# The first two vectors of the adaptive norm: the weights as stationary operand of TensorE, the two conditioning vectors moving, and sixteen places for weight tiles

## Chip, core and metric

The program runs on one core of one Trainium2 chip. The metric is the device time of one execution in microseconds (us). Each engine of the core (TensorE, called PE; its weight loads, PEld; VectorE, DVE; ScalarE, ACT; GpSimd, POOL) takes its instructions in a fixed order, and the SyncE queue (SP) issues the DMAs in a fixed order too: a DMA that has to wait holds up all DMAs behind it.

## What is computed

The reference is a two-layer backbone over 1024 latent tokens and 256 context tokens with 1024 channels. Every sub-layer starts with an RMS norm whose shift and scale come from a conditioning vector. Cut to the part that matters here:

```python
silu_c = jax.nn.silu(c)                # latent tokens, 1024 values
silu_cc = jax.nn.silu(c_ctx)           # context tokens, 1024 values
mod   = silu_c  @ ada_w[i] + ada_b[i]  # ada_w[i]: 1024 x 6144
mod_c = silu_cc @ ada_w[i] + ada_b[i]
sh_m, sc_m, g_m, sh_f, sc_f, g_f = jnp.split(mod, 6, axis=-1)
h = modulate(rmsnorm(x, norm_mix_w[i]), sh_m, sc_m)   # h * (1 + scale) + shift
...
y, y_c = ab_mixer(h, hc, ...)
```

Nothing of layer 0 behind its first norm can start before its scale (vector 1 of the six) and shift (vector 0) are there. Each of these two vectors is a product of two rows of 1024 values with a 1024 x 1024 piece of `ada_w[0]`, 4 MB in float32.

## The kernel before

Activations lie with channels on the 128 partitions and tokens along the free axis, in eight tiles `xT[0..7]`. The large products run in three passes of a split (`whi`, `wlo` times `hh`, `hl`).

The start of the program is what the change touches. `body` calls `setup`, then makes a generator `ada(s, a, 0, [1, 0], "pe")` for vectors 1 and 0, and loads ten row tiles of `x` and `ctx` (`load_x`, 128 tokens x 1024 channels, 512 KB each), taking one step of the generator after each. After row tiles 3, 7 and 9 a block of tokens is turned: `turn_x` transposes, for each of the eight channel groups, the block's row tiles on PE into PSUM (`xt`), and ACT (even groups) and DVE (odd groups) copy the result to `xT`. Then `rstd` squares the eight groups on ACT, adds them on DVE, and sums over partitions with float32 matmuls against one column of ones (`ss`, 128x1). Blocks 0, 1 and 2 hold 512, 512 and 256 tokens.

A step of the generator loads one tile of weights (`adaw`, 128 input channels x 1024 output channels, 512 KB) and multiplies it with the two vectors `cs`. Eight steps (`k` = 0..7) make one vector, so there are sixteen tiles. Before the change, the four columns `cs[:, k, 2 - 2v : 6 - 2v]` (two of them zero) are the stationary operand and half a weight tile moves, 512 columns: the result `adaps` is four rows of 512. It is copied to SBUF (`adarow`), turned by four small transposes (`adat`), sorted (`adasum`), and added to the bias, which gives `mod`.

The weight tiles and the row tiles of x lie in the sixteen places of `hslot` (tags `h0k`, `h1k`; one buffer each), which later hold the normalised activations `hh`, `hl`. Row tile `i` takes place `h(i%2)(i//2)`, so that the row tiles fill places `h00` to `h14`; the weight tiles before take the six places with numbers 5, 6 and 7. A tile framework orders the instructions of each engine by its own simulation and adds the waits.

Behind this stage stands `norm` of block 0 (`spread`: the matmul `rbc`; then per channel group `nt` on DVE, `hh` on ACT with the shift as bias, `hl` on DVE), and behind it the first products `qk`.

Of the kernel before, what the change touches and what calls it, by code (L numbers as in the profile page):

```python
# [11 lines left out]
F32 = mybir.dt.float32  # L12
# [8 lines left out]
P = 128  # L21
D = 1024
KT = D // P
# [46 lines left out]
def psum(s, tag, name=None):  # L70

    if tag == "s" and s.single:
        return s.pp.tile([P, 512], F32, name=name or tag, tag="q", bufs=4)
    if tag != "s":
        return s.ps.tile([P, 512], F32, name=name or tag, tag=tag, bufs=2 if tag == "t" else 1)
    if s.half is None:
        pair = psum2(s, name)
        s.half = pair[:, 512:]
        return pair[:, :512]
    half, s.half = s.half, None  # L80
    return half


def psum2(s, name=None):

    s.half = None
    return s.pp.tile([P, 1024], F32, name=name or "pair", tag="s", bufs=2)
# [25 lines left out]
def setup(s, a):  # L113
    nc, cp = s.nc, s.cp
    cp.tile([P, 24], F32, name="pad")
    s.ident = cp.tile([P, P], F32, name="ident")
    make_identity(nc, s.ident)
    s.ones = cp.tile([P, P], F32, name="ones")
    nc.gpsimd.memset(s.ones, 1.0)
    s.half_neg = cp.tile([P, 16], F32, name="half_neg")  # L120
    nc.gpsimd.memset(s.half_neg, -0.5)


    flat = lambda ap, n: bass.AP(tensor=ap.tensor, offset=ap.offset, ap=[[P, n], [1, P]])
    r0 = s.xp.tile([16, P], F32, name="r0")
    nc.sync.dma_start(r0[0:8, :], flat(a["c"], 8))
    nc.sync.dma_start(r0[8:16, :], flat(a["c_ctx"], 8))
    s.cs = s.hc.tile([P, KT, 6], F32, name="cs")
    nc.gpsimd.memset(s.cs, 0.0)
    pt = psum(s, "t", "setup")  # L130
    nc.tensor.transpose(pt[:, :16], r0, s.ident[:16, :16])
    nc.scalar.activation(s.cs[:, :, 2:4], pt[:, :16].rearrange("p (s k) -> p k s", s=2), AF.Silu)

    r1 = s.xp.tile([P, P], F32, name="r1")
    nc.gpsimd.memset(r1, 0.0)
    rows = [("nmw", a["norm_mix_w"], 16), ("nfw", a["norm_ffn_w"], 16), ("dbf", a["cd_decay_b_fwd"], 2),
            ("dbb", a["cd_decay_b_bwd"], 2), ("hnw", a["cd_head_norm_w"], 1), ("sgb", a["ab_sgu_b"], 4)]
    at = 0
    for name, ap, n in rows:
        nc.sync.dma_start(r1[at:at + n, :], flat(ap, n))  # L140
        at += n
    r2 = s.xp.tile([96, P], F32, name="r2")
    nc.sync.dma_start(r2, flat(a["ada_b"], 96))
    pt = psum(s, "t", "setup")
    nc.tensor.transpose(pt[:, :P], r1, s.ident)
    nc.tensor.transpose(pt[:, P:P + 96], r2, s.ident[:96, :96])
    s.cols = cp.tile([P, 41], F32, name="cols")
    nc.vector.tensor_copy(s.cols, pt[:, :41])
    s.adab = cp.tile([P, 96], F32, name="adab")
    nc.vector.tensor_copy(s.adab, pt[:, P:P + 96])  # L150
    at = 0
    s.col = {}
    for name, ap, n in rows:
        s.col[name] = s.cols[:, at:at + n]
        at += n
    s.mod = [cp.tile([P, 48, 2], F32, name=f"mod{l}") for l in range(2)]
    s.acol = [[cp.tile([P, KT, 2], F32, name=f"acol{l}{j}") for j in range(2)] for l in range(2)]


def ada(s, a, l, vecs, eng):  # L160

    nc = s.nc
    for i, m in enumerate(vecs):
        if eng == "pe":
            acc = psum(s, "o", "adaps")
        else:
            acc = s.adap.tile([P, 2, D], F32, name="adaacc", tag="adaacc", bufs=1)
        for k in range(KT):  # L170
            if eng == "pe":
                w = hslot(s, (8 * i + k) % 2, 5 + (8 * i + k) // 2 % 3, dt=F32, name="adaw")
            else:
                w = s.adap.tile([P, D], F32, name="adaw", tag="adaw", bufs=s.nada)
            nc.sync.dma_start(w, a["ada_w"][l, k * P:(k + 1) * P, D * m:D * (m + 1)])
            for v in range(2):
                c = s.cs[:, k, v + 2:v + 3]
                if eng == "pe":

                    nc.tensor.matmul(acc[:4, :], s.cs[:, k, 2 - 2 * v:6 - 2 * v], w[:, 512 * v:512 * (v + 1)],  # L180
                                     start=k == v == 0, stop=k == KT - 1 and v == 1)
                elif k == 0:
                    nc.scalar.mul(acc[:, v], w, c)
                elif eng == "dve":
                    nc.vector.scalar_tensor_tensor(acc[:, v], w, c, acc[:, v], ALU.mult, ALU.add)
                else:
                    prod = s.adap.tile([P, D], F32, name="adaprod", tag="adaprod", bufs=2)
                    nc.scalar.mul(prod, w, c)
                    nc.gpsimd.tensor_tensor(acc[:, v], acc[:, v], prod, ALU.add)
            if k < KT - 1:  # L190
                yield 1
        sums = s.adap.tile([P, 2, 8], F32, name="adasum", tag="adasum", bufs=1)
        if eng == "pe":
            row = s.adap.tile([4, 512], F32, name="adarow", tag="adarow", bufs=1)
            nc.vector.tensor_copy(row, acc[:4, :])
            pt = psum(s, "m", "adat")
            for q in range(4):
                nc.tensor.transpose(pt[:, 4 * q:4 * q + 4], row[:, P * q:P * (q + 1)], s.ident[:4, :4])
            nc.vector.tensor_copy(sums.rearrange("p v (h q) -> p q h v", h=2), pt[:, :16].rearrange("p (q h v) -> p q h v", q=4, h=2))
        else:  # L200
            for v in range(2):
                for q in range(2):
                    pt = psum(s, "mo"[q], "adat")
                    for j in range(4):
                        c = 4 * q + j
                        nc.tensor.transpose(pt[:, j * P:(j + 1) * P], acc[:, v, c * P:(c + 1) * P], s.ident)
                    nc.vector.tensor_reduce(sums[:, v, 4 * q:4 * q + 4], pt.rearrange("p (j q) -> p j q", j=4),
                                            AX.X, ALU.add)
        nc.vector.tensor_tensor(s.mod[l][:, 8 * m:8 * (m + 1), :], sums.rearrange("p v c -> p c v"),
                                s.adab[:, 48 * l + 8 * m:48 * l + 8 * (m + 1)].rearrange("p (c o) -> p c o", o=1)  # L210
                                .to_broadcast([P, 8, 2]), ALU.add)
        yield 1
# [1533 lines left out]
def hslot(s, x, k, shape=(P, T), dt=F32R, name="hslot"):  # L1746

    return s.hm.tile(list(shape), dt, name=name, tag=f"h{x}{k}", bufs=1)
# [73 lines left out]
def body(ctx, tc, a, out, dbg=None):  # L1822
# [26 lines left out]
    with P_("hc", side="left") as s.hc:  # L1849
# [6 lines left out]
        with ExitStack() as es:  # L1856
# [4 lines left out]
            with R("ld") as ld, R("np0") as s.np_:  # L1861
                s.xp = s.adap = ld
                setup(s, a)
                jobs = [q(0), k(0)]
                s.bg = ada(s, a, 0, [1, 0], "pe")
                xin, r = [], {}
                for i in range(TA // P):
                    xin.append(load_x(s, a, i))
                    tick(s)
                    if i == 7:  # L1870
                        acol(s, 0, 0)
                    if i in (3, 7, 9):
                        blk = BLK[(i - 2) // 3]
                        turn_x(s, xin, xT, blk)
                        r[blk] = rstd(s, xT, blk)
                tick(s, 3)
                ws = proj_w(s, a, jobs)
                drain(s)
                hT = alloc_hc(s)
                s.hc.tile([P, 16], F32, name="pad")  # L1880
                proj_t(s, a, hT, jobs, pre=lambda blk: norm(s, xT, hT, 0, 0, blk, r[blk]), ws=ws)
                spill(s, xT, xd[0])
            with R("ad") as s.adap:
                s.nada = 2
                rbd = s.dp.tile([120, 64, P], F32, name="rbd")

                def prepare():
                    rows = bias_rows(s, a, s.adap, rbd)
                    for i, _ in enumerate(ada(s, a, 0, [2, 3, 4], "dve")):
                        if i % 3 == 2:  # L1890
                            next(rows, 0)
                        yield 1

                s.bg = prepare()
                gmlp(s, a, hT, mixd, q(1), values_b(s, a, hT, vb, 0))
                drain(s)
                acol(s, 0, 1)
# [258 lines left out]
```

## Time and profile before

| what | value |
|---|---|
| time, median of 3 runs | 2769.5 us (2765.0 to 2773.36) |
| the profiled execution, its own time | 2768.02 us |
| its span, first to last instruction | 2766.2 us |
| mean granted TensorE clock | 0.985 |
| DMA, mean over the span | 131 GB/s |
| first `hh` of block 0 (ACT) starts | 59.08 us into the span |

The span is the program's own; the 1.8 us beside it lie around it. A line of the timeline gives start, duration (of the first start to the last end, where several are merged), engine, line, operation, written tile, read tiles, shapes, and how many. A float32 matmul appears as two records, since PE makes two passes; a transpose as one. The 40 slices of the page are too coarse for a stage of 60 us, so the prediction reads windows of a few us.

### The profile page before, as it was taken

The page shows a single profiled execution, that of the slowest core. Times are in us where ns is not written, and L with a number is a line of the kernel's source. Part 1 is how long each engine was busy: PE and PEld are TensorE (multiplying, and loading weights), DVE is VectorE, ACT ScalarE, POOL GpSimd, SP SyncE. Part 2 cuts the span into 40 slices and gives each one's busy share as a digit, 9 for nine tenths or more (in the row PEclk, how much of TensorE's full clock was granted, in tenths as well). Part 3 has the DMA queues.
Part 4 walks back from the last instruction along what each step waited for, and adds up shares of the span by engine and source line. Part 5 has one row for each costly group of instructions (what it writes and reads, how often), then busy time and mean ns, then how long its engine had stood idle before and what let it go on. Part 6 is the DMA issues. An engine that isn't in the chain of part 4 may idle for free.

```text
span 2766.2 us, 39949 instructions
## 1 busy us (share of the span) xinstructions
PE 2654.0 (96%) x14447; PEld 2255.3 (82%) x14447; DVE 1944.8 (70%) x3508; ACT 1022.7 (37%) x2244; POOL 426.4 (15%) x389
## 2 busy tenths in 40 slices
PE   8999899999999999999999988999999999999998
PEld 3889798778888888888888877788877888888887
DVE  4655677776867778778878774756677666677666
ACT  3442466554533333333111145565244222222222
POOL 0000122221212122211000020312002112121111
PEclk9999999999999999999999989999999999999999
DMA  8545665766234434346644242542641111211112
GB/s 312 149 151 140 184 174 138 237 191 195 107 119 137 133 130 139 128 130 227 240 160 149 65 146 86 150 138 71 193 140 46 61 46 46 61 47 61 55 52 84
DMA packets 281590, 361.02 MB, mean 131 GB/s; under 512 B 38008, under 2 KB 198961, under 8 KB 281393
## 3 DMA queue, kind: packets, MB, share of 16 engines
q1 hardware_dynamic: 281393, 358.46, 41.3%
q8 instruction: 115, 1.88, 0.3%
q14 instruction: 82, 0.67, 0.1%
HBM read 259.03 MB, written 95.94 MB: 128 GB/s over the span
## 4 chain that ended last, share of the span: by engine, by line
PE 68%; DVE 14%; DMA 6%; ACT 5%; issue 4%; POOL 2%; SPq 1%; DVEq 0%; POOLq 0%; ACTq 0%
PE dn L49 6%; PE dn L50 6%; PE dn L51 6%; PE qp L49 6%; PE qp L50 6%; PE qp L51 6%; DVE adaacc L231 2%; DMA adaw<-in_ada_w_dram 2%; DVE wlo L57 2%; PE o L1159 2%; PE pt L1129 1%; ACT whi L56 1%; PE ho L49 1%; PE qk L49 1%; PE sp L1070 1%
## 5 line engine op out<-in xcount | busy, mean ns | idle before, releaser
L56 ACT CAST whi<-wraw 128x512 fp32r<-128x512 f32 (+1 forms) x451 | 292.1, 661 | 888.5 <-PE dn L50 375.0
L57 DVE TENSOR_TENSOR wlo<-wraw,whi 128x512 fp32r<-128x512 f32 (+1 forms) x451 | 355.9, 796 | 192.2 <-ACT whi L56 186.7
L351 DVE SCALAR_TENSOR_TENSOR xT<-dn,mod,xT 128x512 f32<-128x512 f32 (+1 forms) x448 | 303.7, 686 | 132.0 <-PE dn L51 130.3
L558 POOL TENSOR_TENSOR wraw<-wraw 128x512 f32<-128x512 f32 x160 | 230.1, 1438 | 897.1 <-DVE wlo L57 710.2
L231 DVE SCALAR_TENSOR_TENSOR adaacc<-adaw,cs,adaacc 128x512 f32<-128x512 f32 x196 | 165.7, 865 | 19.6 <-DMA adaw<-in_ada_w_dram 19.0
L49 PE MATMUL dn<-hhi,whi 128*128 128x512 f32 (+1 forms) x416 | 157.2, 378 | 0.0
L51 PE MATMUL dn<-hhi,wlo 128*128 128x512 f32 (+1 forms) x416 | 156.8, 377 | 0.0
L50 PE MATMUL dn<-hlo,whi 128*128 128x512 f32 (+1 forms) x416 | 156.7, 377 | 0.0
L49 PE MATMUL qp<-hh,whi 128*128 128x512 f32 x320 | 125.3, 391 | 6.8 <-DVE hu L626 6.8
L51 PE MATMUL qp<-sums,wlo 128*128 128x512 f32 x320 | 125.3, 391 | 1.9 <-DVE wlo L57 1.9
L49 PE MATMUL qp<-sums,whi 128*128 128x512 f32 x320 | 124.8, 390 | 0.1
L51 PE MATMUL qp<-hh,wlo 128*128 128x512 f32 x320 | 124.6, 389 | 0.0
L50 PE MATMUL qp<-sums,whi 128*128 128x512 f32 x320 | 124.5, 389 | 0.0
L50 PE MATMUL qp<-hl,whi 128*128 128x512 f32 x320 | 124.5, 389 | 0.0
L626 DVE TENSOR_TENSOR hu<-qp,hu 128x512 f32<-128x512 f32 x120 | 82.5, 687 | 54.2 <-PE qp L51 53.0
L49 PE MATMUL dn<-hslot,whi 128*128 128x512 f32 x288 | 112.3, 390 | 1.1 <-DVE xT L351 1.1
L51 PE MATMUL dn<-hslot,wlo 128*128 128x512 f32 x288 | 112.2, 390 | 0.0
L50 PE MATMUL dn<-hslot,whi 128*128 128x512 f32 x288 | 112.2, 390 | 0.0
L1086 POOL TENSOR_SCALAR y<-y,sst 128x768 f32<-128x768 f32 (+2 forms) x80 | 71.9, 900 | 259.2 <-DVE sst L1085 123.8
L49 PEld LDWEIGHTS dn<-hhi,whi 128*128 128x128 f32 x416 | 78.2, 188 | 14.8 <-ACT hhi L56 0.3
L50 PEld LDWEIGHTS dn<-hlo,whi 128*128 128x128 f32 x416 | 78.2, 188 | 14.4
L49 PE MATMUL cp<-hc,whi 128*128 128x256 f32 x320 | 89.9, 281 | 0.0
(677 smaller groups left out, 7682.2 us busy)
## 6 DMA issues: line engine op xcount, KB each, us to landing
adaw<-in_ada_w_dram SPq DMA_DIRECT2D x112, 256.0 KB, 2.8
wraw<-in_ffn_w_gate_dram SPq DMA_DIRECT2D x44, 512.0 KB, 3.8
wraw<-in_ffn_w_up_dram SPq DMA_DIRECT2D x44, 512.0 KB, 3.8
wraw<-in_ffn_w_down_dram SPq DMA_DIRECT2D x42, 512.0 KB, 3.4
adaw<-in_ada_w_dram SPq DMA_DIRECT2D x40, 512.0 KB, 5.7
xd<-xT SPq DMA_DIRECT2D x24, 640.0 KB, 3.9
xT<-xd SPq DMA_DIRECT2D x48, 256.0 KB, 4.2
wraw<-in_ab_w_in_dram SPq DMA_DIRECT2D x20, 512.0 KB, 5.7
```

The source lines that it names most:

```text
L49: nc.tensor.matmul(out, wh, xh, start=start, stop=False)
L50: nc.tensor.matmul(out, wh, xl, start=False, stop=False)
L51: nc.tensor.matmul(out, wl, xh, start=False, stop=stop)
L56: s.nc.scalar.copy(hi, src)
L57: (s.nc.gpsimd if eng == "pool" else s.nc.vector).tensor_tensor(lo, src, f32(hi), ALU.subtract)
L231: nc.vector.scalar_tensor_tensor(acc[:, v], w, c, acc[:, v], ALU.mult, ALU.add)
L351: s.nc.vector.scalar_tensor_tensor(xT[k][:, o:o + n], ps, s.mod[l][:, 8 * vec + k, sel:sel + 1], xT[k][:, o:o + n], ALU.mult, ALU.add)
L558: sub = lambda out, x, y: feed.s.nc.gpsimd.tensor_tensor(out, x, y, ALU.subtract)
L626: add = lambda out, x, y: nc.vector.tensor_tensor(out, x, y, ALU.add)
L1070: nc.tensor.matmul(sp[:, o:o + n], qq[:, x, :], kk[:, t0:t0 + n], start=x == 0, stop=x == 1)
L1086: nc.gpsimd.tensor_scalar(y[:, :256 + xn], y[:, :256 + xn], st[:, 5:6], 1.0, ALU.mult, ALU.mult)
L1159: nc.tensor.matmul(o_ps[:, ba * P:bz * P], vv[:n, kt, :], at(x, sl)[:n, 0, ba:bz, :].rearrange("p b q -> p (b q)"), start=q == 0 and x == ...
```

## The change

In `ada` with `eng == "pe"`, each 128x128 piece of the weight tile becomes the stationary operand and the two columns of `cs` move. The result has output channels on the partitions and the two vectors beside each other, as `mod` wants it, so that the copy, the four transposes and the sorting go. Vector 1 accumulates in PSUM bank "m", vector 0 in "o". The weight tiles take all sixteen places, in order; the first ten of them are the places of the ten row tiles of x. The clearing of `cs` goes.

```diff
-    nc.gpsimd.memset(s.cs, 0.0)
...
         if eng == "pe":
-            acc = psum(s, "o", "adaps")
+            acc = psum(s, "mo"[i % 2], "adaps")[:, :16].rearrange("p (c v) -> p c v", c=8)
...
             if eng == "pe":
-                w = hslot(s, (8 * i + k) % 2, 5 + (8 * i + k) // 2 % 3, dt=F32, name="adaw")
+                w = hslot(s, k % 2, (8 * i + k) // 2 % 8, dt=F32, name="adaw")
...
-            for v in range(2):
+            for c in range(8 if eng == "pe" else 0):
+                nc.tensor.matmul(acc[:, c, :], w[:, P * c:P * (c + 1)], s.cs[:, k, 2:4], start=k == c == 0,
+                                 stop=k == KT - 1 and c == 7)
+            for v in range(0 if eng == "pe" else 2):
                 c = s.cs[:, k, v + 2:v + 3]
-                if eng == "pe":
-
-                    nc.tensor.matmul(acc[:4, :], s.cs[:, k, 2 - 2 * v:6 - 2 * v], w[:, 512 * v:512 * (v + 1)],
-                                     start=k == v == 0, stop=k == KT - 1 and v == 1)
-                elif k == 0:
+                if k == 0:
...
         if eng == "pe":
-            row = s.adap.tile([4, 512], F32, name="adarow", tag="adarow", bufs=1)
-            nc.vector.tensor_copy(row, acc[:4, :])
-            pt = psum(s, "m", "adat")
-            for q in range(4):
-                nc.tensor.transpose(pt[:, 4 * q:4 * q + 4], row[:, P * q:P * (q + 1)], s.ident[:4, :4])
-            nc.vector.tensor_copy(sums.rearrange("p v (h q) -> p q h v", h=2), pt[:, :16].rearrange("p (q h v) -> p q h v", q=4, h=2))
+            by_c = acc
...
-        nc.vector.tensor_tensor(s.mod[l][:, 8 * m:8 * (m + 1), :], sums.rearrange("p v c -> p c v"),
+        nc.vector.tensor_tensor(s.mod[l][:, 8 * m:8 * (m + 1), :], by_c,
                                 s.adab[:, 48 * l + 8 * m:48 * l + 8 * (m + 1)].rearrange("p (c o) -> p c o", o=1)
                                 .to_broadcast([P, 8, 2]), ALU.add)
```

The SP queue, before, at the end of the row tiles (`adaw` is a weight tile, `xin` a row tile, `wraw` a weight of the first projection, `xd` the spill of `xT`); the rows ahead of it alternate in the same way from the first row tile on:

```order
L261 DMA xin<-in_x_dram 128x1024
L175 DMA adaw<-in_ada_w_dram 128x1024
L261 DMA xin<-in_ctx_dram 128x1024
L175 DMA adaw<-in_ada_w_dram 128x1024
L261 DMA xin<-in_ctx_dram 128x1024
L175 DMA adaw<-in_ada_w_dram 128x1024 x4
L64 DMA wraw<-in_ab_w_in_dram 128x8x128 x2
L175 DMA adaw<-in_ada_w_dram 128x1024 x3
```

After the change, from the first row tile to the end of the weight tiles (the loads of small parameters left out at the mark):

```order
L255 DMA xin<-in_x_dram 128x1024 x4
L139 DMA r_162<-in_norm_mix_w_dram 16x128
...
L255 DMA xin<-in_x_dram 128x1024 x3
L174 DMA adaw<-in_ada_w_dram 128x1024 x4
L255 DMA xin<-in_x_dram 128x1024
L255 DMA xin<-in_ctx_dram 128x1024 x2
L174 DMA adaw<-in_ada_w_dram 128x1024 x9
L64 DMA wraw<-in_ab_w_in_dram 128x8x128 x2
L174 DMA adaw<-in_ada_w_dram 128x1024 x3
```

The first weight tile stands behind seven row tiles now; tiles 0 to 3 of the weights take places that row tiles 0 to 3 hold, and the first of them waits for PE. Of the nine in the next group, tiles 10 and 11, which have free places, go first; tiles 4 to 9 take the places of row tiles 4 to 9.

PE from the row tiles of block 1 that are turned early, past the sum of block 0 (`ss`), to the turn of block 1, after the change, with what each row waits for (left out at the marks: the rest of a group, and tile 2):

```order
L266 MATMUL xt<-ident,xin 128x128 [waits DMAHW7_49]
...
L308 MATMUL ss<-ones,sqacc 128x1 [waits DVE_49]
...
L176 MATMUL adaps<-cs,adaw 128x2 [waits DMAHW0_49]
L176 MATMUL adaps<-cs,adaw 128x2 x7
L176 MATMUL adaps<-cs,adaw 128x2 [waits DMAHW1_49]
...
L176 MATMUL adaps<-cs,adaw 128x2 [waits DMAHW3_49]
...
L266 MATMUL xt<-ident,xin 128x128 [waits DMAHW4_49]
```

Four whole weight tiles stand between the sum of block 0 and the turn of block 1. Before the change, pairs of wide matmuls stood singly between the transposes, from the first row tile on. The other twelve tiles stand behind block 1: tile 4 within the last transposes of block 2, then tile 5, the sum of block 1, tiles 6 and 7, the sum of block 2, `rbc`, and tiles 8 to 15 in a row.

The end of the stage on DVE, before:

```order
L195 COPY adarow<-adaps 4x512
L330 SCALAR_TENSOR_TENSOR nt<-xT_131,acol_182,rbc 128x512
L199 COPY adasum<-adat 128x4x2x2
L330 SCALAR_TENSOR_TENSOR nt<-xT_132,acol_182,rbc 128x512
L209 TENSOR_TENSOR mod_180<-adasum,adab 128x16
L339 SCALAR_TENSOR_TENSOR hl_513<-nt,mod_180,hh_512 128x512
```

and after:

```order
L324 SCALAR_TENSOR_TENSOR nt<-xT_131,acol_181,rbc 128x512
L324 SCALAR_TENSOR_TENSOR nt<-xT_132,acol_181,rbc 128x512
L57 TENSOR_TENSOR wlo<-wraw,whi 128x1024 x2
L203 TENSOR_TENSOR mod_179<-adaps,adab 128x16
L333 SCALAR_TENSOR_TENSOR hl_590<-nt,mod_179,hh_589 128x512
```

The shift (`mod`) comes straight from PSUM, and both `nt` and the two splits of the first projection's weights stand ahead of it.

More of the change, by code (lines that the diff above doesn't have):

```diff
@@ L191, in ada @@
                 yield 1
-        sums = s.adap.tile([P, 2, 8], F32, name="adasum", tag="adasum", bufs=1)
         if eng == "pe":
-            row = s.adap.tile([4, 512], F32, name="adarow", tag="adarow", bufs=1)
-            nc.vector.tensor_copy(row, acc[:4, :])
-            pt = psum(s, "m", "adat")
-            for q in range(4):
-                nc.tensor.transpose(pt[:, 4 * q:4 * q + 4], row[:, P * q:P * (q + 1)], s.ident[:4, :4])
-            nc.vector.tensor_copy(sums.rearrange("p v (h q) -> p q h v", h=2), pt[:, :16].rearrange("p (q h v) -> p q h v", q=4, h=2))
-        else:
+            by_c = acc
+        else:
+            sums = s.adap.tile([P, 2, 8], F32, name="adasum", tag="adasum", bufs=1)
+            by_c = sums.rearrange("p v c -> p c v")
             for v in range(2):
```

## Prediction

> **What bounds the kernel now.** I read the page first: PE is busy 96% of the span, and the chain of work that ended last lies on it for two thirds.
>
> ```profile
> PE 2654.0 (96%) x14447; PEld 2255.3 (82%) x14447; DVE 1944.8 (70%) x3508; ACT 1022.7 (37%) x2244; POOL 426.4 (15%) x389
> PE 68%; DVE 14%; DMA 6%; ACT 5%; issue 4%; POOL 2%; SPq 1%; DVEq 0%; POOLq 0%; ACTq 0%
> ```
>
> So a delay at the start of the program is carried to its end, unless work behind it has slack. The stage of the change ends with the first `hh`; its end on the chain, and the timeline of the small operations that the change removes or keeps there:
>
> ```profile
> 52.85 3.53 PE adaps L180 x8
> 56.38 1.07 PE rbc L296 x2
> 57.47 0.75 DVE nt L330
> 58.38 0.49 issue
> 59.08 0.73 ACT hh L338
> ...
> 56.41 0.68 DVE L195 COPY adarow<-adaps 4x512 f32<-4x512 f32 x1 [3.37 <-PE adaps L180]
> 57.36 0.41 PE L198 MATMUL adat<-ident,adarow 4*128 4x4 f32 x4
> 58.87 0.17 DVE L209 TENSOR_TENSOR mod<-adasum,adab 128x16 f32<-128x16 f32 x1
> ```
>
> PE's wide `adaps` matmuls end at 56.4 us, and 2.7 us later `hh` starts. Next the timeline of the SP queue and the windows of the DMA:
>
> ```profile
> 1.87 0.43 SPq L261 DMA_DIRECT2D xin<-in_x_dram  x1
> ...
> 23.19 8.64 SPq L175 DMA_DIRECT2D adaw<-in_ada_w_dram  x4
> 35.17 6.94 SPq L175 DMA_DIRECT2D adaw<-in_ada_w_dram  x3
> ...
> 0.00:5.00 5.00, 0.25 (x1) 0.17 (x1) 0.00 (x0) 1.47 (x2) 1.10 (x10) 1.00 0.44 137
> 5.00:10.00 5.00, 1.92 (x5) 0.67 (x6) 0.00 (x0) 0.00 (x0) 0.00 (x0) 1.00 0.84 312
> 20.00:25.00 5.00, 5.00 (x22) 1.85 (x20) 3.44 (x7) 3.47 (x6) 0.00 (x0) 1.00 1.02 414
> ...
> DMA to landing us min/median/max: 3.3/6.2/10.3
> ```
>
> (A window's columns are its length, busy time with counts of PE, PEld, DVE, ACT and POOL, granted clock, DMA share, GB/s; the last row is that of `xin`.) At 414 GB/s one 512 KB tile (0.524 MB) takes 1.27 us. Now the price of the old product, from the groups of 0 to 75 us and two timeline rows:
>
> ```profile
> L180 PE MATMUL adaps<-adaw,cs 128*4 128x512 f32 x64 | 32.5, 630 | 0.0
> 9.38 4.95 PE L180 MATMUL adaps<-adaw,cs 128*4 128x512 f32 x6
> 29.59 1.88 PE L180 MATMUL adaps<-adaw,cs 128*4 128x512 f32 x4
> ```
>
> Four passes in 1.88 us with 0.59 us for the last one's own length: 0.43 us a pass, 64 passes 27.5 us. The first six needed twice as long a step: PE starts at half clock and leaves it at about 14 us, though the clock column prints 1.00 there. The step between passes is the safer reading.
>
> **The change, part by part.** *New product.* 16 tiles x 8 pieces x 2 passes = 256 passes, each with its own 128-column weight load and 2 moving columns. The trace has nearly this form: `ss`, 128x128 stationary, one column moving. At full and at half clock:
>
> ```profile
> 28.61 1.05 PE L314 MATMUL ss<-ones,sqacc 128*128 128x1 f32 x8 [0.18 <-DVE sqacc L310]
> 28.00:32.00 4.00, 3.66 (x18) 1.62 (x16) 1.41 (x3) 0.23 (x1) 1.03 (x1) 1.00 1.03 410
> 1609.96 1.87 PE L314 MATMUL ss<-ones,sqacc 128*128 128x1 f32 x8 [3.89 <-POOL sqacc L310]
> 1608.00:1612.00 4.00, 1.87 (x8) 1.78 (x8) 0.14 (x1) 1.55 (x4) 3.09 (x4) 0.50 1.01 393
> ...
> L314 PE MATMUL ss<-ones,sqacc x20: 250/250/271, 28.6 to 52.6; 128*128 128x1 f32 x20
> ```
>
> With 0.25 us for the last pass at full clock and 0.36 at half, a step is 0.8/7 = **0.114 us** at full clock and 1.51/7 = **0.216 us** at half. So 256 passes cost 29.2 us or 55.3 us, against 27.5 now: the new form saves PE nothing even at its best, and the clock decides. A tile costs 1.83 or 3.45 us.
>
> [...]
>
> *Which clock.* Here I looked for a stretch at half clock in which narrow passes fill PE, and found one, at the grid on which the clock's records change (3.41 us):
>
> ```profile
> 2080.83 1.70 PE L407 MATMUL ss<-ones,nt 128*128 128x1 f32 x8
> 2078.95:2082.36 3.41, 3.41 (x13) 2.93 (x13) 0.00 (x0) 0.51 (x1) 0.00 (x0) 0.50 0.00 0
> 2082.36:2085.77 3.41, 3.41 (x9) 2.73 (x10) 2.91 (x6) 0.00 (x0) 1.40 (x1) 0.50 0.12 24
> 2085.77:2089.18 3.41, 3.41 (x14) 2.45 (x14) 2.15 (x4) 1.01 (x2) 1.19 (x1) 1.00 0.87 267
> ```
>
> PE has no pause in the first window, almost half of it narrow, and the clock stays at half; only after a window of wide passes alone is it full. Transposes (their count in the stage, then a stretch of others at half clock) didn't lift it either:
>
> ```profile
> L272 PE MATMUL xt<-ident,xin 128*128 128x128 f32 x80 | 13.3, 293 | 6.3 <-DMA xin<-in_x_dram 5.2 <-ACT xT L276 1.1
> 288.14 1.97 PE L206 MATMUL adat<-ident,adaacc 128*128 128x128 f32 x8 [4.47 <-DVE adaacc L185]
> 290.36:293.77 3.41, 2.52 (x11) 2.12 (x11) 2.76 (x7) 0.65 (x2) 0.00 (x0) 0.50 0.90 217
> 293.77:297.18 3.41, 1.79 (x3) 1.01 (x4) 1.49 (x3) 1.04 (x1) 0.00 (x0) 0.50 0.59 177
> ```
>
> In the changed program no wide matmul but `rbc` stands ahead of `qk`; what lifted the clock at 14 us, the wide `adaps`, is gone. I take half clock for the whole stage: 55.3 us for the product, and for transposes the same step (the 8 at 288.14 take 1.97 us with the last one's length), 1.73 us for 8.
>
> *Queues and places.* The sixteen places don't free the loads: the first ten are held by row tiles until turned. Step by step, in us:
>
> - Row tiles 0 to 3 (2.1 MB) have landed at about 10.0, by the two windows (0.69 + 1.56 MB). Block 0 turns in four rounds of 8 transposes on PE with copies behind them, an estimate of 1.9 a round (1.73 and a short wait): first copy at 10.4, last transposes at 16.1. SP waits with weight tile 0 as soon as row tiles 4 to 6 are issued, and issues it at 16.1.
>
> ```profile
> 18.11 0.59 ACT xT L276
> ```
>
> - Now block 0 takes from this first copy to `ss` at 28.61, thus 10.5 us; with no weights between I take 10: `ss` at 20.4, until 22.3.
> - Weight tiles 0 to 3 land from 19.4 (16.1 + 3.3) to 23.2; four tiles at 3.45 keep PE until 36.1. Then block 1: three rounds behind its last row tile and the squares on ACT between them, 42.5. Only now SP issues tile 4, which lands at about 45.5.
> - 13 transposes of block 2 until 46.5, tile 4 until 50.0, three transposes 50.7, tile 5 54.2, `ss` 56.1, tiles 6 and 7 63.0, `ss` 63.9, `rbc` (two wide passes) 65.7, tiles 8 to 15 93.3. Their last load: tile 8 is issued at 50.7, and eight loads at 1.27 with 3.3 to land end at 64: hidden by PE.
>
> *The tail.* `adarow`, `adat` and `adasum` go (between 56.4 and 59.1), and `mod` with 0.17 us reads PSUM: `hh` 0.3 us behind the last pass, at 93.6. This gives back about 2.4 us, contained in the sum. The cleared `cs` was off the path.
>
> *Cover.* `wraw`, its splits, both `nt` and the spills of `xT` lie beside PE's 27 us of tiles 8 to 15. If that cover were gone, the two splits at most would show. Behind `hh` the program is as before, and `qk` starts in part at half clock already now, so that no second loss comes from there:
>
> ```profile
> 60.00:65.00 5.00, 4.72 (x13) 3.54 (x14) 4.87 (x8) 1.93 (x4) 0.00 (x0) 0.67 0.65 217
> ```
>
> **Sum:** 93.6 - 59.1 = +34.5 us. The profiled execution took 2768.0 (span 2766.2 and 1.8 around it), 1.5 below the runs' median: 2768.0 + 34.5 = 2802.5, forecast **2802**.
>
> Ends: PE's own work at half clock is 55.3 + 80 transposes 17.3 + 20 passes of `ss` 4.3 + `rbc` 1.8 = 78.7; from 10.0 without one wait it ends at 88.7, +29.9. Above, some 5 us more waiting for loads or copies: +40. With full clock throughout the same walk gives tiles 0 to 3 until 28.6, block 1 33.9, tile 4 at 37.0, tiles 8 to 15 from 47.3 to 62, `hh` 62.3: +3.
>
> **Rivals.**
> 1. *Not slower: the clock is lifted.* The narrow passes count as activity: from the first four tiles on, PE runs at full clock. For it: PE would have no pause for 27 us. Against: the window at 2078.95. Time 2768.0 + 3 = 2771, within the noise. It decides when a stretch of narrow passes alone of some 7 us shows steps of 0.114.
>    [...]
> 2. *Lifted in parts.* The turns of blocks 0 and 1 pack transposes closer than at 288 (2.52 of 3.41 us), and lift the clock for one or two windows each, until narrow windows drop it: 3.4 us saved for each two windows, some 7 in all: 2795.
> 3. *The places help after all*, and weights arrive with no stall of SP: PE alone then sets the end, +29.9: 2798. It lies in the range.
> 4. *Faster.* For `hh` at 51 the full-clock walk ends 11 us too late: its 29.2 us would have to be 18, or 0.07 us a pass; no row shows that.
>
> **Chances.** Forecast with rival 3: 0.73; rival 2: 0.12; rival 1: 0.12; faster: 0.02; worse than the range: 0.01. The range 2788 to 2810 takes in rivals 2 and 3 and the waits above. A measurement of this kernel tells about 0.3% (8 us) from no change: faster 0.02, same 0.12, slower 0.86.
>
> **What would show it.** In the profile after: `ss` of block 0 (8 passes) in 1.87 us, not 1.05; 16 passes of a tile in 3.45, not 1.83; SP waiting on PE for weight tile 0 until about 16 and for tile 4 until about 42; the first `hh` at 93 to 94; everything behind shifted alike. Steps of 0.114 in tiles 8 to 15 would prove the clock step wrong, a first `hh` above 100 the walk through the queue, and an `hh` shift that the end doesn't show would prove slack behind the stage.

## The result and the profile after

The changed kernel took 2805.9 us in the median of four runs (2799.7 to 2809.2), the kernel before, in four runs beside them, 2770.3 us (2765.0 to 2773.4). The ratio is **1.0124, 95% interval 1.0108 to 1.014**: slower by 30 to 39 us. The forecast of 2802 us lies 4 us below the median and inside the range given.

The profiled execution of after is its fastest run, 2799.7 us (span 2797.9), 31.7 us above the profiled one of before. First the timeline of PE in the stage (start, length from the first start to the last end, line, operation, output and inputs, shapes, count; in brackets the idle time ahead and what ended it):

```profile
21.30 1.50 PE L308 MATMUL ss<-ones,sqacc 128*128 128x1 f32 x8 [3.01 <-DVE sqacc L304]
22.66 13.79 PE L176 MATMUL adaps<-cs,adaw 128*128 128x2 f32 x64
...
37.44 5.32 PE L266 MATMUL xt<-ident,xin 128*128 128x128 f32 x24 [0.46 <-ACT xT L270]
...
46.58 1.84 PE L176 MATMUL adaps<-cs,adaw 128*128 128x2 f32 x16
49.54 3.41 PE L176 MATMUL adaps<-cs,adaw 128*128 128x2 f32 x16
52.81 1.84 PE L308 MATMUL ss<-ones,sqacc 128*128 128x1 f32 x8
54.52 6.97 PE L176 MATMUL adaps<-cs,adaw 128*128 128x2 f32 x32
64.81 27.31 PE L176 MATMUL adaps<-cs,adaw 128*128 128x2 f32 x128
```

Read the steps: 16 passes in 3.41 us (tile 5) are 0.213 us each, 16 passes in 1.84 us (tile 4) 0.112. The same instruction runs at two speeds, and most of it at the slow one: the last 128 passes take 27.31 us without a pause. Then the tail of the stage and the SP queue:

```profile
92.15 0.17 DVE L203 TENSOR_TENSOR mod<-adaps,adab 128x16 f32<-128x16 f32 x1 [23.42 <-PE adaps L176]
92.36 1.33 ACT L332 ACTIVATE hh<-nt,mod 128x512 fp32r<-128x512 f32 x2 [31.06 <-DVE mod L203]
...
16.37 1.75 SPq L174 DMA_DIRECT2D adaw<-in_ada_w_dram  x4
42.47 8.38 SPq L174 DMA_DIRECT2D adaw<-in_ada_w_dram  x7
```

The first `hh` starts at 92.36 instead of 59.08, **33.3 us later**. Behind it stand 2705.5 us to the end of the span, before 2707.1: in these two executions the loss lies in this stage alone, and nothing behind it gives it back. (In the other profiled runs below this rest took 2706 to 2718 us, so differences of a few us in the time of a program can't be put down to the stage; the first `hh` is the finer measure.) SP issues weight tile 0 at 16.4 and tile 4 at 42.5, each behind the turn of a block.

The windows show the clock (columns: window; its length; busy time and count of PE, PEld, DVE, ACT, POOL; granted clock; DMA share; GB/s):

```profile
11.46:14.87 3.41, 3.40 (x16) 2.77 (x16) 1.98 (x3) 2.39 (x5) 0.00 (x0) 1.00 0.80 239
14.87:18.28 3.41, 2.61 (x18) 1.75 (x16) 2.96 (x7) 1.89 (x5) 0.00 (x0) 1.00 0.41 117
18.28:21.69 3.41, 0.40 (x5) 0.39 (x4) 2.65 (x4) 1.71 (x3) 0.00 (x0) 1.00 1.00 378
21.69:25.11 3.42, 3.42 (x18) 3.42 (x18) 0.85 (x2) 0.00 (x0) 1.03 (x1) 0.51 1.01 395
25.11:28.52 3.41, 3.41 (x18) 3.41 (x17) 0.00 (x0) 0.00 (x0) 0.00 (x0) 0.50 1.03 411
38.76:42.18 3.42, 3.42 (x17) 2.52 (x16) 2.58 (x4) 2.50 (x5) 0.00 (x0) 0.50 0.00 0
42.18:45.59 3.41, 2.38 (x15) 1.41 (x14) 2.86 (x5) 2.56 (x6) 0.00 (x0) 0.99 0.59 187
65.00:92.00 27.00, 27.00 (x129) 27.00 (x127) 3.68 (x4) 0.00 (x0) 0.00 (x0) 0.50 0.45 180
```

PE is without a pause from 65 to 92 and the clock stays at 0.50. A window full of transposes (38.76) is followed by full clock, the windows of narrow passes (21.69, 25.11 and the two after them, to 35.35) by none. One trap: the trace's first clock record is at 14.9, and the column prints 1.00 ahead of it; the transposes of the first row here are 0.21 apart, so that stretch ran at half clock too.

### The profile page after: what moved, and what is told of

Same layout as the page of the kernel before. It is cut to its first block, busy times and chain, and to the rows that moved or that the text cites. A ratio compares the mean times of both kernels' runs of the same rounds, so it can differ in the third digit from the quotient of the medians.

```text
span 2797.9 us, 40309 instructions
## 1 busy us (share of the span) xinstructions
PE 2680.9 (96%) x14631; PEld 2308.9 (83%) x14631; DVE 1947.9 (70%) x3504; ACT 1022.7 (37%) x2244; POOL 425.7 (15%) x388
## 4 chain that ended last, share of the span: by engine, by line
PE 67%; DVE 13%; DMA 7%; ACT 5%; issue 4%; POOL 2%; SPq 1%; DVEq 0%; POOLq 0%; ACTq 0%
PE dn L49 6%; PE dn L51 6%; PE dn L50 6%; PE qp L49 6%; PE qp L50 6%; PE qp L51 6%; DMA adaw<-in_ada_w_dram 3%; DVE wlo L57 2%; DVE adaacc L225 2%; PE adaps L176 2%; PE o L1153 2%; PE pt L1123 1%; ACT whi L56 1%; POOL wraw L552 1%; DMA wraw<-in_ffn_w_gate_dram 1%
## 5 line engine op out<-in xcount | busy, mean ns | idle before, releaser
L51 PEld LDWEIGHTS dn<-hhi,wlo 128*128 128x128 f32 x416 | 78.3, 188 | 14.2
```

Source lines behind the costliest of these rows:

```text
L51: nc.tensor.matmul(out, wl, xh, start=False, stop=stop)
```

## Experiments

Three theories stood against each other. **Clock**: passes that move two columns neither raise nor keep TensorE's clock. **Places**: the sixteen places, of which the first ten hold row tiles, make SP wait, and that is the loss. **Pace**: 256 passes with 256 weight loads are slow by themselves, whatever the clock does.

### The two halves of the change apart

Narrow passes in the old places (edit to the changed kernel):

```diff
-                w = hslot(s, k % 2, (8 * i + k) // 2 % 8, dt=F32, name="adaw")
+                w = hslot(s, (8 * i + k) % 2, 5 + (8 * i + k) // 2 % 3, dt=F32, name="adaw")
```

> The changed product (weights stationary, two moving columns) with the six old places for its weight tiles, so that their loads no longer wait for row tiles and the scheduler mixes tiles with transposes as before. Clock theory (narrow passes leave TensorE at half clock): PE's own work of 78.7 us from about 10 on sets the end, first hh at 85 to 89, time 2795 to 2800; passes 0.213 us apart in most windows. Places theory (the wait of SP for row tiles is the loss): the loss goes, first hh at 58 to 62, time 2769 to 2773.

Wide passes in the new places: the opposite edit, made to the kernel before.

> The old product (vectors stationary, 512 columns move, with its tail) in the sixteen new places, where the first ten hold row tiles. Clock theory: the wide passes lift the clock, the waits of SP until about 16 and 42 us remain, but cost only what the walk at full clock gave, +3, and the old tail's 2.4: first hh at 62 to 66, time 2772 to 2777. Places theory: the loss of the changed kernel stays, first hh at 88 to 93, time 2797 to 2806.

The rows of the first run, then of the second:

```profile
88.58 1.33 ACT L332 ACTIVATE hh<-nt,mod 128x512 fp32r<-128x512 f32 x2 [14.47 <-DVE mod L203]
29.59 3.41 PE L176 MATMUL adaps<-cs,adaw 128*128 128x2 f32 x16
10.00:30.00 20.00, 19.54 (x92) 18.51 (x92) 3.82 (x8) 4.97 (x9) 0.00 (x0) 1.00 1.00 376
```

```profile
69.48 1.33 ACT L338 ACTIVATE hh<-nt,mod 128x512 fp32r<-128x512 f32 x2 [17.48 <-DVE mod L209]
52.88 13.90 PE L180 MATMUL adaps<-adaw,cs 128*4 128x512 f32 x32
```

Narrow passes in the old places: 2802.4 us against 2775.3 of the kernel before on that chip, ratio 1.0086 (1.0065 to 1.0107), first `hh` 29.5 us later than before, in the range of the clock theory. SP's waits for row tiles are gone, and of the delay of `hh` nine tenths stay, of the loss of time three quarters (27 of 36 us, each beside its own runs of the kernel before). PE has almost no pause; its 256 passes are 54.6 us busy and never reach full clock (against the 1.00 in the window: 92 passes and transposes in 19.54 us are 0.21 each, and the wide passes of `qk` behind them are 0.43 apart until 95.43 and 0.23 from 95.78 on).

Wide passes in the new places: 2780.6 us, ratio 1.0017 (1.0005 to 1.0029), first `hh` 10.4 us later. So the places theory can't carry the loss. But the places do cost something, and more than the 3 to 7 us expected of `hh`; that the measured time rose only by 1 to 8 us for it isn't explained by what was run. With narrow passes they cost 3.8 us of `hh` (92.36 against 88.58), or 6.3 against the 94.86 of a later run of the changed kernel. That this is less than 10.4 because PE at half clock has work left while the loads come is an argument, not shown.

### The same passes, more columns

If the clock is the cause, more moving columns must make the kernel *faster*. The two vectors are repeated by an operand with stride 0; passes, weight loads and places stay. With 64 columns (8 x 64 = 512) one `psum` tile of the kernel, 512 columns, still holds a vector, and the weight tiles keep their order on PE. With 128 each vector fills two of them, banks "m" and "o", `mod` is added in two halves (128x8), and the scheduler chose another order: tiles 4 to 7 in a row, the sum of block 1, tile 8, the sum of block 2, `rbc`, tiles 9 to 15.

```diff
-            acc = psum(s, "mo"[i % 2], "adaps")[:, :16].rearrange("p (c v) -> p c v", c=8)
+            acc = psum(s, "mo"[i % 2], "adaps").rearrange("p (c r v) -> p c r v", c=8, r=32)
...
-                nc.tensor.matmul(acc[:, c, :], w[:, P * c:P * (c + 1)], s.cs[:, k, 2:4], start=k == c == 0,
-                                 stop=k == KT - 1 and c == 7)
+                nc.tensor.matmul(acc[:, c], w[:, P * c:P * (c + 1)],
+                                 s.cs[:, k, 2:4].rearrange("p (o v) -> p o v", o=1).to_broadcast([P, 32, 2]),
+                                 start=k == c == 0, stop=k == KT - 1 and c == 7)
...
-            by_c = acc
+            by_c = acc[:, :, 0, :]
```

> The changed kernel with the two vectors repeated 32 times as moving operand: 64 columns move a pass in place of 2, everything else (256 passes, weight loads, order, places) the same. If columns that move are what keeps the clock, and half of a transpose's 128 are enough: passes 0.114 us apart, first hh about 62 to 66, time 2771 to 2776. If they are not enough: 0.213 us apart and 2800 to 2807 as changed. Theory that the weight loads or the number of instructions set the pace: no change, 2800 to 2807.

> The same with the vectors repeated 64 times: 128 columns move a pass, as in a transpose, into two banks; 256 passes and weight loads as changed. Clock theory: the clock rises during the first four weight tiles and stays up, passes 0.114 us apart, first hh at 62 to 68, time 2771 to 2777, although more is moved. Theory that the weight loads or the number of instructions set the pace, whatever moves: 0.213 us apart, time 2800 or more.

Timeline and windows with 64 columns:

```profile
23.31 13.89 PE L176 MATMUL adaps<-cs,adaw 128*128 128x64 f32 x64
57.48 14.51 PE L176 MATMUL adaps<-cs,adaw 128*128 128x64 f32 x128 [0.35 <-DMA adaw<-in_ada_w_dram]
72.23 1.33 ACT L333 ACTIVATE hh<-nt,mod 128x512 fp32r<-128x512 f32 x2 [7.64 <-DVE mod L204]
23.52:26.94 3.42, 3.42 (x17) 3.42 (x18) 0.82 (x2) 0.00 (x0) 1.03 (x1) 0.50 1.02 416
40.59:44.00 3.41, 3.41 (x16) 2.51 (x15) 2.33 (x5) 2.82 (x6) 0.00 (x0) 0.50 0.00 0
58.00:72.00 14.00, 13.98 (x126) 13.84 (x124) 3.02 (x3) 2.09 (x2) 0.00 (x0) 1.00 1.06 358
```

And with 128:

```profile
69.12 1.34 ACT L339 ACTIVATE hh<-nt,mod 128x512 fp32r<-128x512 f32 x2 [15.47 <-DMA xd<-xT]
23.91 8.90 PE L176 MATMUL adaps<-cs,adaw 128*128 128x128 f32 x64
23.67:27.08 3.41, 3.41 (x17) 3.41 (x18) 0.85 (x2) 0.00 (x0) 1.03 (x1) 0.50 1.03 414
27.08:30.49 3.41, 3.41 (x32) 3.41 (x32) 0.00 (x0) 0.00 (x0) 0.00 (x0) 1.00 1.02 413
```

With 128 columns one full window of passes brings the clock up, in the middle of the first 64 passes, and it is up at their end (57 to 69 us: 107 passes in 12.00 us at 1.00); `hh` comes 23.2 us earlier than in the changed kernel, although 64 times as much moves. (Some 0.9 us of this is the form's: the first `hh` needs only the first half of `mod`, and so only the first bank.) The time is 2784.2 us, ratio 1.0037 (1.0022 to 1.0053): 7 us above the end of what the clock theory said, of which 5 are the chip's (the kernel before took 2775.3 there, 2770.3 in the first comparison); `hh` is 1 us above. The pace theory falls: with the clock up the same weight loads are 0.112 us apart. The 64-column passes gave an answer between the two expected: they didn't raise the clock in the first 13.89 us (transposes did, to 1.00 at 44.0), but they kept it, 128 passes in 14.51 us at 1.00, and with the order and the bank of the changed kernel `hh` comes at 72.23, 20.1 us earlier. The program took 2786.8 us, ratio 1.0051 (1.0028 to 1.0074), with single runs up to 2807. The longer ones have the lower mean clock (0.974 at 2807.3, 0.978 at 2796.6 and 2794.3, 0.981 to 0.983 in the others); that the transposes failed to raise it there fits this, but isn't shown, as one run is profiled.

### Both costs away

128 columns in the old places, wide passes with the sixteen places in another order (the six that hold no row tile first), both together, and the changed kernel again, on one chip. The edit of the order:

```diff
-                w = hslot(s, (8 * i + k) % 2, 5 + (8 * i + k) // 2 % 3, dt=F32, name="adaw")
+                w = hslot(s, k % 2, ((8 * i + k) // 2 + 5) % 8, dt=F32, name="adaw")
```

> The 128-column form (weights stationary, vectors repeated 64 times) with the six old places, so that both costs seen so far are taken away: half clock, and the waits of SP for row tiles. If these two are all that the change lost, the stage is as short as before the change: 29.2 us of passes for 27.5, the old tail of 2.4 us gone, first hh at 58 to 61 (59.08 before), ratio 0.998 to 1.002. If the weight loads of 256 passes cost more than that, or the copies between them, first hh above 64 and a ratio above 1.002.

> The old wide product with sixteen places, of which the six that no row tile holds are given out first, so that no weight load waits for another weight tile's passes and the first six wait for nothing. If the places themselves bring something once SP doesn't stall: loads arrive earlier, first hh at 55 to 58, ratio 0.997 to 0.999. If TensorE's work sets the end in the old kernel already: first hh at 58 to 60, ratio 0.999 to 1.001.

> The 128-column form with the sixteen places, free ones first. If TensorE's work sets the end: as with the six old places, first hh within 1 us of that run. If the loads do: 2 us or more earlier. If the sixteen places are what hurts, in whatever order: first hh at 66 or later, as with 128 columns in the new places (69.12).

> The changed kernel as it is, beside the others on one chip: first hh at 92 to 93 and a ratio of 1.011 to 1.014 if the loss belongs to the kernel; a ratio near the 1.0086 of the narrow passes in the old places if that difference of 0.4 % was the chip's.

| kernel | median us | ratio (interval) | first `hh` |
|---|---|---|---|
| 128 columns, old places | 2768.5 | 0.999 (0.9982 to 0.9999) | 56.62 |
| wide, sixteen places, free first | 2770.9 | 0.9996 (0.9985 to 1.0007) | 59.59 |
| 128 columns, sixteen places, free first | 2772.0 | 1.0004 (0.9993 to 1.0015) | 59.56 |
| changed kernel again | 2807.7 | 1.0131 (1.0116 to 1.0146) | 94.86 |

The kernel before took 2771.0 us beside them. With the clock up and SP free the whole loss is gone: the two costs account for all of it. The first `hh` is even 2.5 us earlier than before the change (56.62 against 59.08), 1.4 us below the range expected; the time falls by as much, with an interval that ends just short of 1. The changed kernel's own ratio, 1.0131, is as expected (its `hh` 1.9 us above), so by that expectation the 1.0086 of the narrow passes in the old places wasn't the chip's, and with narrow passes the new places cost time as well. The sixteen places bring nothing in either form. In the third kernel `hh` is 2.9 us later than in the first, which none of its expectations had. Its rows, then those of the first, show why:

```profile
51.38 6.50 PE L176 MATMUL adaps<-cs,adaw 128*128 128x128 f32 x56
57.72 1.02 PE L297 MATMUL rbc<-diag,ones 128*128 128x512 f32 x2
59.56 1.38 ACT L339 ACTIVATE hh<-nt,mod 128x512 fp32r<-128x512 f32 x2 [7.89 <-DVE nt L331]
```

```profile
50.89 1.02 PE L297 MATMUL rbc<-diag,ones 128*128 128x512 f32 x2
51.75 5.52 PE L176 MATMUL adaps<-cs,adaw 128*128 128x128 f32 x48
56.41 0.17 DVE L206 TENSOR_TENSOR mod<-adaps,adab 128x8 f32<-128x8 f32 x1 [3.06 <-PE adaps L176]
56.62 1.33 ACT L339 ACTIVATE hh<-nt,mod 128x512 fp32r<-128x512 f32 x2 [6.89 <-DVE mod L206]
57.30 0.17 DVE L206 TENSOR_TENSOR mod<-adaps,adab 128x8 f32<-128x8 f32 x1 [0.73 <-PE adaps L176]
```

The scheduler put `rbc` behind the last passes instead of ahead of them, so `rbc` and `nt`, which lay beside the passes, now follow them. Before the change `rbc` stood behind the last passes too (56.38), beside the old tail: taking the tail away paid here only where `rbc` also came ahead. And of the 2.5 us of the first kernel 0.9 are due to the two halves of `mod`: `hh` starts behind the first (56.41), while the second half can be added only at 57.30, behind the product's last passes.

### How many columns raise it, how many keep it

Three single executions, all on the 128-column form in the new places; the number of columns a pass is changed for tiles 8 to 15 or for all, as here for 32 (64 and 16 repetitions of two columns):

```diff
-                nc.tensor.matmul(acc[c // 4][:, c % 4], w[:, P * c:P * (c + 1)],
-                                 s.cs[:, k, 2:4].rearrange("p (o v) -> p o v", o=1).to_broadcast([P, 64, 2]),
+                rep = 16 if i else 64
+                nc.tensor.matmul(acc[c // 4][:, c % 4, :rep], w[:, P * c:P * (c + 1)],
+                                 s.cs[:, k, 2:4].rearrange("p (o v) -> p o v", o=1).to_broadcast([P, rep, 2]),
```

> Vector pair 1 (tiles 0 to 7) moves 128 columns and brings the clock up; pair 2 (tiles 8 to 15) moves 16, without a pause. If a clock once up is held by anything that keeps TensorE without a pause: 128 passes 0.112 us apart, 14.4 us. If the columns that move decide: the clock drops one or two windows of 3.4 us into the 16-column passes, which then are 0.213 apart, 22 to 27 us in all.

> The same with 32 columns for the second pair. 64 columns held the clock and didn't raise it, 2 didn't hold it. If the limit for holding is near 64: drops as with 16. If it is low: held, 14.4 us for the 128 passes.

> All passes move 96 columns, in the new places. 128 raised the clock in two windows, 64 didn't in four. If the share of time in which columns move decides between these: 96 is either enough (passes 0.112 us apart before the first 64 are over, first hh at 68 to 71) or not (0.213 us for all of the first 64, 13.7 us or more, first hh at 71 to 75).

A row each of the first two, then the third (timeline, then windows):

```profile
54.73 23.91 PE L177 MATMUL adaps<-cs,adaw 128*128 128x16 f32 x112
```

```profile
54.40 23.99 PE L177 MATMUL adaps<-cs,adaw 128*128 128x32 f32 x112
```

```profile
22.34 9.95 PE L177 MATMUL adaps<-cs,adaw 128*128 128x96 f32 x64
...
41.15 1.92 PE L177 MATMUL adaps<-cs,adaw 128*128 128x96 f32 x16
...
50.78 14.50 PE L177 MATMUL adaps<-cs,adaw 128*128 128x96 f32 x128
24.35:27.76 3.41, 3.41 (x18) 3.41 (x17) 0.24 (x1) 0.00 (x0) 0.00 (x0) 0.50 1.03 420
27.76:31.17 3.41, 3.41 (x32) 3.41 (x32) 0.00 (x0) 0.00 (x0) 0.00 (x0) 1.00 0.52 204
```

16 and 32 columns: 112 passes at 0.214 us, the clock down (first `hh` at 77.2 and 76.9; 2797.0 and 2796.3 us, with 2778.5 for the kernel before). 96 columns: raised after one full window, 2778.3 us; `hh` at 64.6 is 3 us earlier than expected. This program has the changed kernel's order on PE again (tile 4 alone at 41.15, tiles 8 to 15 in a row), so that its last 128 passes start at 50.8, where the 128-column kernel, in its other order, still has 112 to do at 57.0. But in the first two the clock fell in a window that also had a pause of PE, so one more run put two 128-column tiles ahead of the narrow ones:

```diff
-                rep = 16 if i else 64
+                rep = 16 if i and k > 1 else 64
```

> Tiles 0 to 9 move 128 columns, tiles 10 to 15 (96 passes behind tile 9, with no pause planned) 32. In the runs with 16 and 32 columns for all of tiles 8 to 15 the clock fell in a window that also had a pause, so that it isn't shown what narrow passes alone do to a clock that is up. If narrow passes let it fall by themselves: 0.112 us a pass for one or two windows of 3.4 us, then 0.213, the 96 passes in 13 to 18 us. If only the pause did it: 0.112 to the end, 10.8 us, first hh at 65 to 70.

```profile
56.74:60.15 3.41, 3.41 (x34) 3.41 (x32) 0.00 (x0) 0.00 (x0) 0.00 (x0) 1.00 1.03 428
60.15:63.57 3.42, 3.42 (x33) 3.42 (x33) 0.00 (x0) 0.00 (x0) 0.00 (x0) 1.00 1.01 418
63.57:66.98 3.41, 3.41 (x18) 3.41 (x18) 0.00 (x0) 0.00 (x0) 0.00 (x0) 0.50 1.02 422
```

The count of PE in each row is the reading: 34, 33, then 18 passes in the same time, PE busy throughout. The first row still holds about a microsecond of 128-column passes; the second is the first window of narrow ones alone, and at its end the clock falls. The 96 passes behind tile 9 took some 15 us (to 72.95), as expected of passes that let it fall, and the first `hh` comes at 71.5; the run took 2782.9 us, with 2777.4 for the kernel before. So in this run 32-column passes by themselves let the clock fall, without a pause.

## Why the prediction was right, and where it wasn't

**The clock step** carries the result. It said 0.216 us a pass and 55.3 us in all. The group of the stage (busy time, mean ns of one):

```profile
L176 PE MATMUL adaps<-cs,adaw 128*128 128x2 f32 x256 | 53.3, 345 | 0.0
L266 PE MATMUL xt<-ident,xin 128*128 128x128 f32 x80 | 18.2, 371 | 8.8 <-DMA xin<-in_x_dram 5.1 <-ACT xT L270 2.6 <-DVE xT L268 1.1
L308 PE MATMUL ss<-ones,sqacc 128*128 128x1 f32 x20 | 4.4, 336 | 3.6 <-DVE sqacc L304 3.6
```

53.3 us, with 0.213 a pass at half clock (16 x 8 matmuls left 256 records of passes and 256 of weight loads, two of each for one matmul; the 80 transposes left 80 passes). The form with one moving column (`ss`) was the right stand-in for one with two.

**Rival 1's argument**, no pause of PE for 27 us, held, and the clock didn't rise: in the window 65.00:92.00 two-column passes keep PE busy for 27.00 of 27.00 us at 0.50, and 64 columns left it at half for 13.89 us. With 96 and 128 columns one full window of 3.41 us was enough.

**The walk through the queue** held to half a microsecond at most steps up to tile 4: weight tile 0 issued at 16.4 (16.1 said), tiles 0 to 3 done at 36.5 (36.1), tile 4 issued at 42.5 (42.5), its passes from 46.6 (46.5). One step was off by more and was made up by luck: the sum of block 0 began at 21.3 (20.4 said), but in a window at full clock, so that tile 0 could follow at 22.7 (22.3).

**The tail** was sized rightly: from the end of the passes to `hh` it is 0.24 us (92.12 to 92.36), where it was 2.7 before the change. That the 128-column form in the old places beats the kernel before by 2.5 us is not the same thing, though the numbers are alike: its passes end 0.9 us later than the old ones (57.27 against 56.38), and its `hh` doesn't wait for the last of them.

**"Transposes ... didn't lift it either" was too strong.** It rested on a stretch where transposes fill 2.52 of 3.41 us. The turns of blocks 0 and 1 fill a whole window (3.40 of 3.41 us and 3.42 of 3.42), and both lifted the clock, for two windows each (full from 14.9 to 21.7 and from 42.2 to 49.0): the lift that rival 2 describes. Its price was too high, not its direction: only part of `ss` (1.50 for 1.87 us), a few transposes and tile 4 (1.84 for 3.45 us) fell into the lifted windows, and the first `hh` came 1.2 us before the walk's 93.6, not 7. When the changed kernel ran again, transposes still reached full clock (five in 0.77 us at 17.70, four in 0.65 at 45.69, as in the lifted windows of the first execution), but the lift was over sooner: `ss` took 1.87 us, tile 4 3.41, both at half clock, and `hh` came at 94.86.

**Rival 3's price** (+29.9 without SP's waits) was met by the narrow passes in the old places, +29.5; its condition, that the sixteen places help, wasn't met by any run.

**Rival 1's price** (+3 at full clock) was too low: in the changed kernel's order, with 96 columns, `hh` comes 5.5 us later than before, with 128 columns 10.0. The failing term of the walk is its start at full clock: with 96 columns tiles 0 to 3 end at 32.3 instead of 28.6, as the clock rises only at 27.8, and tile 4 begins about as much later (41.15 for 37.0). With 128 columns the sum of block 0 began 1.4 us later still (22.18 for 20.75), and most of what is left comes with the other order of that program:

```profile
42.58 7.31 PE L176 MATMUL adaps<-cs,adaw 128*128 128x128 f32 x64
54.66 0.61 PE L315 MATMUL ss<-ones,sqacc 128*128 128x1 f32 x4 [1.98 <-DVE sqacc L311]
57.00 12.77 PE L176 MATMUL adaps<-cs,adaw 128*128 128x128 f32 x112 [0.77 <-DMA adaw<-in_ada_w_dram]
```

Four tiles stand behind the transposes at once, the sum of block 2 then keeps PE waiting for 1.98 us, and one load, costed as hidden, is late. This didn't touch the forecast, but it shows that the places would have cost even a product that keeps the clock.

## What to carry to other kernels

Before a product with few moving columns is turned to stationary weights, ask what holds the clock around it: here 256 passes at 0.112 us each would be some 29 us at full clock, an estimate, and kept PE busy for 54.6 at half, and with 32, 16 and 2 columns a pass the clock ended at half. Moving the same columns again through a stride-0 operand costs nothing in the steps measured here (0.112 us with 2, 64, 96 and 128 columns at full clock), and with 64, 96 and 128 columns the clock stayed up (1.00 over 12 to 14 us). The SP queue, which issues in order, stood still here at places that a row tile still held (weight tile 0 issued at 16.4 us, tile 4 at 42.5; in the profile after it waited for transposes for 32.8 us in all, 21.3 at the longest): the order in which places are given out can cost more than their number brings (10.4 us of `hh` for the wide product here, nothing gained with the free ones first).

## What was not expected of the hardware

Passes of the same pace did different things to the clock, and keeping it up took fewer moving columns than raising it. In fp32 with 128-column weights: 96 and 128 moving columns raised it after one full window of 3.41 us, 64 kept it (14 us at 1.00) but didn't raise it (13.9 us), 32 let it fall after one window of nothing else. Each but the 128 is from one profiled execution. Passes that move more columns also write more into PSUM (128x2 to 128x128 here), and no run tells these two apart. And the clock column prints 1.00 ahead of a trace's first clock record (14.9 us in the profile after): the narrow passes in the old places show a mean clock of 0.986 in a run whose passes stood 0.21 us apart, as at half clock, through the whole stage. The step between passes is the safer reading.
